# Column sums by 32x32 transposes, fewer norm sums, a new opening and end, and one weight sum moved from VectorE to GpSimd in an encoder block

## Chip, cores and metric

The kernel runs on one core of a Trainium2 chip. The metric is the device time of one execution in microseconds (us). PE is TensorE, DVE is VectorE, ACT is ScalarE, POOL is GpSimd, SP is SyncE, which issues most DMAs.

## What is computed

One block of an encoder on x (1024 positions x 1024 channels, float32), conditioned by a vector c:

```python
ada = silu(c) @ w_ada + b_ada                     # 1024 -> 6 x 1024
shift1, scale1, gate1, shift2, scale2, gate2 = split(ada, 6)
h = rmsnorm(x, g_mix) * (1 + scale1) + shift1
qa, ka, va, qb, kb, vb, ga, gb = split(h @ w_in)  # 512 x6, 1024 x2
oa = mixture_of_dilations(qa, ka, va, rel_bias)   # branch A, 3 window patterns
ob = neighbourhood_attention_2d(qb, kb, vb, rpb)  # branch B
x = x + gate1 * ((sigmoid(ga) * (oa @ w_branch_dil) + sigmoid(gb) * (ob @ w_branch_na)) @ w_out)
h2 = rmsnorm(x, g_ffn) * (1 + scale2) + shift2
u_val, u_gate = split(depthwise_conv3(h2 @ w_up))
x = x + gate2 * ((gelu(u_gate) * u_val) @ w_down)
return rmsnorm(x, g_final)
```

with rmsnorm(x, g) = x * rsqrt(mean(x*x) + 1e-6) * g.

## The kernel before

Activations lie with channels on the partitions: a tile is 128 channels x 512 positions, eight channel tiles (index k or m) by two halves of the positions (`hf`). Every large product is made of three fp32r matmuls: weights and activations are split into a high part (an ACT copy to fp32r, `whi`, `h`) and a low part (a subtraction on POOL or DVE, `wlo`), and high x high, high x low and low x high are added up in PSUM. So PE does most of the work, and ACT, DVE and POOL make its operands.

The stages, in order: the opening (norm of x's first half, the first columns of ada, products for q, k, v of the first heads); v and q/k products of the second half, with the remaining columns of ada summed beside them; attention, where the projections of later heads are woven between the softmax and value matmuls; the gating of the two branches (`w_br`); `w_out` with the norm for the FFN; `w_up` with seven products per 2x2 blocks (Strassen's scheme; `STEPS`, the sums of weights S1 to S4 and of activations T1 to T4), convolution and gelu; `w_down`; and the end with the last norm.

**Column sums.** Sums over partitions are done by PE: `add_sums` (L104) takes a 128x512 tile of squares as the stationary operand, in four blocks of 128 columns, and a column of ones as the moving one; four plain fp32 matmuls (eight records in the trace) give 512 sums, one per position, laid over the partitions. `rstd_of` (L110) makes the reciprocal root of them (DVE, ACT, DVE), and `bcast` (L118) turns it by four transposes into a 128x512 tile `pbc` that DVE multiplies with. Where squares are kept in two accumulators, there are two sets of four. The norm of half 1 does so (`square`, `square_sums`, L201 to L217), `out_tile` for half 0 (its last square apart), and the end (`late`: the sum, m=6 and m=7).

The columns of ada come the same way: `row_pairs` (L555) multiplies rows of `w_ada` by elements of silu(c) and adds them up on DVE into `sums[j]` (a 128x512 tile for each j from 4 to 9, whose 128 partitions are still to be summed), and two steps later `ada_sums` (L170) sums over the partitions with four matmuls against ones, and `ada_bias` (L177) adds the bias on DVE. In the `w_br` stage `row_add` (L1205) does the same for j = 10 and 11.

**Opening.** `warm` issues filler matmuls (L246) until the first data are there. DVE computes 1/D * sum + eps, ACT the root, DVE the reciprocal; ACT copies the turned factor to SBUF (`pbs`), so that POOL may scale x tiles 2 to 7 while DVE scales 0 and 1. The order of all engines in this stage is the order of the code (`manual_schedule`).

**k eviction.** `k_evict` (L370) copies k from PSUM for two heads: `one` is ACT's scaled copy (L381), `two` DVE's low part (L385) and the DMAs to the other 64 partitions. In attention both are put on a list of side work by `later` with a credit in ns, and are issued between the steps of the softmax: scores plus bias on DVE with the row maximum (L672), exp on ACT (L673), turning on PE, copies of the turned tile on ACT (L680, `th`) and DVE (L681, `tl`), then PE again (L795 for the first pattern). In branch B the two heads are put as `later(750, one for head 0)` and `later(750, one for head 1, two for both heads)`. Weight splits (L730 on ACT, L731 on POOL) are side work as well.

**w_up's first tiles.** Each step's weights go through `a_operands` (L1261), a generator: POOL makes S1, S2 and S3 (L1273 to L1275), ACT and POOL split the pairs, DVE makes S4 = a12 - S2 (L1291). `gens` holds the product generators of the first three tiles; the first products need only half 0 of the activations, while half 1 is normed: L113, `bcast` (L121), then DVE scales `m2[k]` (L1640), and forms the sums for T2, T1 and so on (L1643 on) in an order that is written out by hand for ACT, DVE and POOL.

**End.** Three chunks (half 0, and two quarters) get their last products, squares (ACT, L1794), sums on POOL for m < 6 (L1798), `add_sums`, `rstd_of`, `bcast`; a chunk's scaling (L1775) is done in the next chunk's loop. For the last chunk DVE scales all eight tiles (L1814), and four DMAs of 256 KB store them (L1819).

## Time and profile before

| | us |
|---|---|
| median of 3 runs | 1493.36 (1491.71 to 1493.61) |
| profiled execution: its own time | 1490.45 |
| its span in the trace | 1488.6 |
| mean granted TensorE clock | 0.996 |
| DVE / ACT / POOL busy | 935.8 / 773.6 / 763.2 |

In a row of the timeline stand the start, the duration of the group of like instructions (x gives their count), the engine, the line, the operation with its output and inputs, and in brackets the idle time ahead of it and what ended it. Matmuls overlap, so their cadence is read from their starts. In a row of the stages stand the length, then for PE, weight loads, DVE, ACT and POOL the busy time and the count, then the granted clock, the share of the DMA engines and GB/s. A row of groups ends with busy time and mean duration in ns.

### The profile page before, as it was taken

To read this page: it belongs to the slowest core of one execution; us is meant where nothing else is said; L and a number is where in the kernel's file an instruction comes from. 1 tells how busy PE (TensorE), PEld (TensorE's weight loads), DVE (VectorE), ACT (ScalarE), POOL (GpSimd) and SP (SyncE) were. 2 spreads that over 40 slices of the span, in tenths; PEclk is the share of its full clock that TensorE was granted. 3 is DMA by queue.
4 is the path that set the end of the run, shared out by engine and by line. 5 is a ranking of instruction groups with operands and counts; after the bars stand their busy time and mean duration, and the time that the engine had idled before them with its cause. 6 is when DMAs were issued, how large, how long until landed. Compare 5 with 4: busy or idle time off the path is not lost.

```text
span 1488.6 us, 21635 instructions
## 1 busy us (share of the span) xinstructions
PE 1471.5 (99%) x7652; PEld 1252.7 (84%) x7652; DVE 935.8 (63%) x1760; ACT 773.6 (52%) x1442; POOL 763.2 (51%) x635
## 2 busy tenths in 40 slices
PE   9999999999999999999999999999999999999997
PEld 8888888889798998888888778888888888878887
DVE  7783546555555666566515897666666667887865
ACT  5522666666655666653345464444444447485542
POOL 4131332433234354422268668766766676988711
PEclk9999999999999999999999999999999999999998
DMA  9587233445645556577544314222222234542313
GB/s 367 195 303 258 73 97 87 139 108 140 160 148 140 152 156 170 164 259 254 193 152 140 105 43 141 86 85 81 82 70 84 73 133 141 198 141 72 110 36 114
DMA packets 117301, 210.29 MB, mean 141 GB/s; under 512 B 42788, under 2 KB 55716, under 8 KB 117156
## 3 DMA queue, kind: packets, MB, share of 16 engines
q1 hardware_dynamic: 115192, 205.95, 43.2%
q10 hardware_dynamic: 2000, 2.95, 0.5%
q8 instruction: 60, 0.98, 0.3%
q14 instruction: 49, 0.40, 0.1%
HBM read 163.58 MB, written 42.66 MB: 139 GB/s over the span
## 4 chain that ended last, share of the span: by engine, by line
PE 86%; DVE 4%; POOL 3%; DMA 2%; issue 2%; ACT 2%; SPq 0%; DVEq 0%; POOLq 0%; ACTq 0%
PE pj L1326 11%; PE pj L1325 11%; PE pj L1324 11%; PE pj L84 11%; PE pj L86 10%; PE pj L85 10%; PE pj L414 3%; PE O L1027 2%; PE T L1014 1%; PE S L992 1%; PE pv L289 1%; PE pv L291 1%; PE pv L290 1%; PE O L858 1%; PE O L807 1%
## 5 line engine op out<-in xcount | busy, mean ns | idle before, releaser
L61 POOL TENSOR_TENSOR wlo<-wraw,whi 128x512 fp32r<-128x512 f32 (+1 forms) x84 | 106.2, 1287 | 146.1 <-ACT whi L57 145.9
L84 PE MATMUL pj<-h,whi 128*128 128x512 f32 x432 | 178.3, 413 | 0.1
L86 PE MATMUL pj<-h,wlo 128*128 128x512 f32 x432 | 170.0, 394 | 0.0
L85 PE MATMUL pj<-h,whi 128*128 128x512 f32 x432 | 169.6, 392 | 0.0
L1324 PE MATMUL pj<-op,wsh 128*128 128x512 f32 x408 | 159.1, 391 | 1.4 <-ACT op L1254 0.6
L1325 PE MATMUL pj<-op,wsh 128*128 128x512 f32 x408 | 159.0, 390 | 0.9 <-DVE op L1255 0.6
L1326 PE MATMUL pj<-op,wsl 128*128 128x512 f32 x408 | 157.6, 389 | 0.0
L681 DVE TENSOR_TENSOR tl<-T,th 128x512 fp32r<-128x512 f32 (+3 forms) x120 | 77.2, 654 | 106.7 <-ACT th L680 105.4
L731 POOL TENSOR_TENSOR wlo<-wraw,whi 128x512 fp32r<-128x512 f32 x58 | 74.3, 1294 | 125.7 <-ACT whi L730 125.7
L61 POOL TENSOR_TENSOR wsl<-big,wsh 128x512 fp32r<-128x512 f32 (+1 forms) x86 | 111.8, 1323 | 42.5 <-ACT wsh L57 37.6
L673 ACT ACTIVATE P<-P,st 128x256 f32<-128x256 f32 x128 | 64.2, 502 | 93.3 <-DVE st L672 93.3
L1561 DVE SCALAR_TENSOR_TENSOR big<-pj,sm,big 128x512 f32<-128x512 f32 (+2 forms) x183 | 94.9, 563 | 16.5 <-ACT big L1555 15.6
L86 PEld LDWEIGHTS pj<-h,wlo 128*128 128x128 f32 x432 | 81.1, 188 | 18.0
L1324 PEld LDWEIGHTS pj<-op,wsh 128*128 128x128 f32 x408 | 76.6, 188 | 19.3 <-ACT wsh L57 1.5
L1325 PEld LDWEIGHTS pj<-op,wsh 128*128 128x128 f32 x408 | 76.6, 188 | 18.1 <-DVE op L1255 1.2
L84 PEld LDWEIGHTS pj<-h,whi 128*128 128x128 f32 x432 | 81.6, 189 | 11.5 <-issue 0.5
L1325 PE MATMUL pj<-op,whi 128*128 128x512 f32 x232 | 90.4, 390 | 0.0
L1326 PE MATMUL pj<-op,wlo 128*128 128x512 f32 x232 | 90.3, 389 | 0.0
L1324 PE MATMUL pj<-op,whi 128*128 128x512 f32 x232 | 90.2, 390 | 0.0
L85 PEld LDWEIGHTS pj<-h,whi 128*128 128x128 f32 x432 | 81.8, 189 | 10.0
L1326 PEld LDWEIGHTS pj<-op,wsl 128*128 128x128 f32 x408 | 76.6, 188 | 16.0 <-POOL wsl L61 0.3
L61 POOL TENSOR_TENSOR wsl<-wraw,wsh 128x384 fp32r<-128x384 f32 (+1 forms) x46 | 57.3, 1268 | 62.0 <-ACT wsh L57 54.5
(403 smaller groups left out, 4171.7 us busy)
## 6 DMA issues: line engine op xcount, KB each, us to landing
wraw<-w_in SPq DMA_DIRECT2D x32, 512.0 KB
wada<-w_ada SPq DMA_DIRECT2D x31, 512.0 KB
big<-w_up SPq DMA_DIRECT2D x22, 512.0 KB
wraw<-w_up SPq DMA_DIRECT2D x22, 512.0 KB
big<-as SPq DMA_DIRECT2D x22, 512.0 KB
as<-big SPq DMA_DIRECT2D x21, 512.0 KB
gs<-gs SPq DMA_DIRECT2D x32, 256.0 KB
g<-gs SPq DMA_DIRECT2D x16, 512.0 KB
```

The costliest lines, as they stand in the source:

```text
L61: lo_eng.tensor_tensor(lo[:, i:i + step], raw[:, i:i + step], f(hi)[:, i:i + step], OP.subtract)
L84: pe.matmul(psum, whi[:, k0 + k], mhi, start=k == 0, stop=False)
L85: pe.matmul(psum, whi[:, k0 + k], mlo, start=False, stop=False)
L86: pe.matmul(psum, wlo[:, k0 + k], mhi, start=False, stop=k == n - 1)
L414: pe.matmul(p[:, 256 * r:256 * r + 256], ww[:, k], m[:, r], start=k + x + r == 0, stop=k == KT - 1 and x == 2, skip_group_check=True)
L673: act.activation(pp, pp, AF.Exp, bias=mi, scale=-1.0, accum_out=li)
L681: dve.tensor_tensor(tl[:m, :n], pt[:m, :n], f(th)[:m, :n], OP.subtract)
L731: pool.tensor_tensor(lo[:, i:i + n], raw[:, i:i + n], f(hi)[:, i:i + n], OP.subtract)
L1324: pe.matmul(psum, whi[:, k], bhi, start=j < 4 and k == 0, stop=False, skip_group_check=True)
L1325: pe.matmul(psum, whi[:, k], blo, start=False, stop=False, skip_group_check=True)
L1326: pe.matmul(psum, wlo[:, k], bhi, start=False, stop=k == n - 1, skip_group_check=True)
L1561: dve.scalar_tensor_tensor(y[:, dst], src, wt, y[:, dst], OP.mult, OP.add)
```

## The change

1. Column sums of ada (j = 4 to 9 and 10, 11): the partitions are summed in two steps. `fold` turns the 128x512 sum in 32x32 blocks on DVE (a transpose) and reduces the 32 elements of each block's rows to one (128x16). `folds_in` makes a 128x32 matrix `pick` once, by a reduce over the identity. `fold_bias` sums the four groups of 32 partitions with four matmuls, for all six j at once (32x24) at the end of the stage, or for one j (32x4) in `w_br`. The adds of the bias become one for j = 4 to 9.
2. Norms: the squares of half 1 in the early stage go into one accumulator (one set of four matmuls instead of two), as do those of half 0 in `w_out` (one DVE add more for m = 7) and m = 6 at the end for the first two chunks.
3. Opening: 35 filler matmuls instead of 38; eps is a tile, added by the root's bias on ACT, so that DVE's scaling of the sum goes; ACT copies the turned factor ahead of the second half of a weight split; DVE scales x tile 1 behind the first bias.
4. `k_evict` in branch B: `two` is split by head, with a further entry of credit 400.
5. `w_up`: tile 1's S4 is made by POOL, ahead of the split of S3; the factor of half 1 is turned as soon as tile 0's products are issued that far, not three steps of tile 1 later.
6. End: eps as the root's bias; for the last chunk the factor is turned a second time into `bc2`, ACT copies it to SBUF and scales x tiles 4 and 5, POOL multiplies these two, DVE scales the other six; tiles 6 and 7 are stored one by one, and ACT's queue stores 4 and 5.

The core of the diff:

```diff
+    def fold(dst, acc, tmp):
+        dve.transpose(tmp, acc)
+        dve.tensor_reduce(dst, tmp.rearrange("p (c i) -> p c i", i=32), mybir.AxisListType.X, OP.add)
+    def folds_in(tile, n):
+        pick, sums = tile[:, 0:32], tile[:, 32:32 + 16 * n].rearrange("p (j x) -> p j x", j=n)
+        dve.tensor_reduce(pick, idt.rearrange("p (b i) -> p i b", i=32), mybir.AxisListType.X, OP.add)
+        return pick, sums
+    def fold_bias(c0, n, pa, pick, sums):
+        for q in range(4):
+            pe.matmul(pa[32 * q:32 * q + 32, :4 * n], pick, sums.rearrange("p j (m q) -> p (j m) q", q=4)[:, :, q],
+                      start=True, stop=True, skip_group_check=True)
+        ada_bias(c0, pa, 4 * n)
...
-            later(750, lambda: one((1,)), two)
+            later(750, lambda: one((1,)), lambda: two((0,)))
+            later(400, lambda: None, lambda: two((1,)))
...
-        warm(38, idle, True)
+        warm(35, idle, True)
...
-        dve.tensor_scalar(r, every(pcol), 1.0 / D, EPS, OP.mult, OP.add)
-        act.activation(r, r, AF.Sqrt)
+        act.activation(r, every(pcol), AF.Sqrt, bias=eps, scale=1.0 / D)
...
-        pcol = square_sums(accs, lambda: v_products(1, (1,), range(8)))
+        v_products(1, (1,), range(8))
+        pcol = ps_n.tile([128, KT], FT, name="pcol")
+        add_sums(pcol, sqa, True, True)
...
+                if i == 3:
+                    fold(folds[1][:, j - 4], sums.pop(j), early.tile([128, 512], FT, name="mt", bufs=3))
...
-            for j in due.pop(n, ()):
-                ada_bias(4 * j, ada_sums([(sums.pop(j), ones)]))
-            due[n + 2] = [j for j in range(4, 10) if done_rows < 4 * j - 12 <= row_ends[n]]
...
-        for j in sum(due.values(), []):
-            ada_bias(4 * j, ada_sums([(sums.pop(j), ones)]))
+        fold_bias(16, 6, ps_s.tile([128, 512], FT, name="pada", bufs=1), *folds)
...
+        if s4_at == 3:
+            pool.tensor_tensor(S4, a12, S2, OP.subtract)
...
-        if 0 < m < KT - 1:
-            (dve if hf and m > 2 else pool).tensor_tensor(sqa, sqa, sq, OP.add)
+        if 0 < m < KT - 1 or m and hf == 0:
+            (dve if hf and m > 2 or m == KT - 1 else pool).tensor_tensor(sqa, sqa, sq, OP.add)
...
-    prep.append(a_operands(raw.pop(1), 4, s_home, sts[1], dve, spot=extra))
+    prep.append(a_operands(raw.pop(1), 4, s_home, sts[1], dve, spot=extra, s4_at=3))
...
     advance(gens[0])
-    for _ in range(3):
-        next(gens[1])
     bc = bcast(rstd_of(pcol, 4), ps, "pbc")
...
-                elif m < 6:
+                elif m < (7 if cs.start == 0 else 6):
                     pool.tensor_tensor(sqa, sqa, sq, OP.add)
...
+            act.activation(r, pcol[:, :n // 128], AF.Sqrt, bias=eps, scale=1.0 / D)
+            dve.reciprocal(r, r)
...
+        bc2 = bcast(r, ps, "pj", 2, 6)[:, :n]
...
+        for m in (4, 5):
+            act.activation(xs[m], xs[m], AF.Copy, scale=g_fin[:, m:m + 1])
+        act.activation(bs, bc2, AF.Copy)
...
+        for i in range(2):
+            pool.tensor_tensor(ys[4][:, i], xs[4 + i], bs, OP.mult)
...
+        for m in (0, 1, 2, 3, 6, 7):
...
+            dve.scalar_tensor_tensor(yy, xs[m], g_fin[:, m:m + 1], bc, OP.mult, OP.mult)
```

What this moves on the engines, at three places. First, DVE at the end of the early stage, where it sums the last rows of ada (`sq` is such a sum, `wada` the rows); before:

```order
L567 SCALAR_TENSOR_TENSOR sq_1170<-wada_1122,cs_65,sq_1170 128x512 x2
L565 TENSOR_SCALAR sq_1243<-wada_1126,cs_65 128x512
L567 SCALAR_TENSOR_TENSOR sq_1243<-wada_1126,cs_65,sq_1243 128x512
L567 SCALAR_TENSOR_TENSOR sq_1243<-wada_1164,cs_65,sq_1243 128x512 x2
L177 TENSOR_TENSOR ada_70<-pada_1251,sm_64 128x4
L567 SCALAR_TENSOR_TENSOR sq_1243<-wada_1168,cs_65,sq_1243 128x512
L1457 TENSOR_TENSOR am1_71<-ada_70 128x4
L567 SCALAR_TENSOR_TENSOR sq_1243<-wada_1168,cs_65,sq_1243 128x512
L567 SCALAR_TENSOR_TENSOR sq_1243<-wada_1173,cs_65,sq_1243 128x512 x2
L177 TENSOR_TENSOR ada_70<-pada_1317,sm_64 128x4
L177 TENSOR_TENSOR ada_70<-pada_1325,sm_64 128x4
L620 SCALAR_TENSOR_TENSOR am2_72<-ada_70,sm_64 128x8
```

and after, with the line numbers of the changed kernel (L575 and L577 are the sums, `mt_821` holds `pick` and the folded sums):

```order
L181 STREAM_TRANSPOSE mt_1233<-sq_1166 128x512
L182 TENSOR_REDUCE mt_821<-mt_1233 128x16
L575 TENSOR_SCALAR sq_1236<-wada_1125,cs_65 128x512
L577 SCALAR_TENSOR_TENSOR sq_1236<-wada_1125,cs_65,sq_1236 128x512
L577 SCALAR_TENSOR_TENSOR sq_1236<-wada_1157,cs_65,sq_1236 128x512 x2
L577 SCALAR_TENSOR_TENSOR sq_1236<-wada_1164,cs_65,sq_1236 128x512 x2
L577 SCALAR_TENSOR_TENSOR sq_1236<-wada_1169,cs_65,sq_1236 128x512 x2
L181 STREAM_TRANSPOSE mt_1273<-sq_1236 128x512
L182 TENSOR_REDUCE mt_821<-mt_1273 128x16
L177 TENSOR_TENSOR ada_70<-pada_1309,sm_64 128x24
L628 SCALAR_TENSOR_TENSOR am2_72<-ada_70,sm_64 128x8
```

Between the sums the small bias adds are gone, a fold (L181, L182) stands behind each finished sum, and one bias add of 24 columns is left. On PE at this place, among the v products (`pv`), before:

```order
L291 MATMUL pv_1361<-vwh_194,h_792 128x512
L289 MATMUL pv_1361<-vwh_194,h_796 128x512
L290 MATMUL pv_1361<-vwl_195,h_796 128x512
L170 MATMUL pada_1325<-ones_68,sq_1243 128x1 x4
L291 MATMUL pv_1361<-vwh_194,h_797 128x512
L289 MATMUL pv_1361<-vwh_194,h_801 128x512
```

and after:

```order
L295 MATMUL pv_1345<-vwh_194,h_785 128x512
L296 MATMUL pv_1345<-vwl_195,h_785 128x512
L297 MATMUL pv_1345<-vwh_194,h_786 128x512
L192 MATMUL pada_1309<-mt_821 32x24 x4
L295 MATMUL pv_1345<-vwh_194,h_790 128x512
L296 MATMUL pv_1345<-vwl_195,h_790 128x512
```

The group L192 needs the last fold; the set it replaces needed the last sum.

Second, DVE in attention, at the k eviction of branch B (`kl` are the low parts of k, `P` the scores); before:

```order
L681 TENSOR_TENSOR tl_4159<-T_4153,th_4158 128x512
L385 SCALAR_TENSOR_TENSOR kl_3687<-pj_4062,ks_3685 64x2x256
L385 SCALAR_TENSOR_TENSOR kl_3688<-pj_4062,ks_3686 64x2x256
L672 ISA P_4179,st_3678<-S_4178,bias_3870 128x256
L672 ISA st_3678 128x1
L672 ISA P_4179,st_3678<-S_4178,bias_3870 128x256
L672 ISA st_3678 128x1
L933 TENSOR_TENSOR u23_2895<-u23_2895,fb_4050 128x512
L681 TENSOR_TENSOR tl_4208<-T_4202,th_4207 128x512
```

and after (L391 is the eviction, L680 the softmax, L689 the turned tile's low part):

```order
L689 TENSOR_TENSOR tl_4143<-T_4137,th_4142 128x512
L391 SCALAR_TENSOR_TENSOR kl_3671<-pj_4046,ks_3669 64x2x256
L680 ISA P_4158,st_3662<-S_4157,bias_3854 128x256
L680 ISA st_3662 128x1
L680 ISA P_4158,st_3662<-S_4157,bias_3854 128x256
L680 ISA st_3662 128x1
L941 TENSOR_TENSOR u23_2879<-u23_2879,fb_4034 128x512
L391 SCALAR_TENSOR_TENSOR kl_3672<-pj_4046,ks_3670 64x2x256
L689 TENSOR_TENSOR tl_4192<-T_4186,th_4191 128x512
```

The second low part stands five rows later, behind a softmax and an add. On ACT at this place (`whi` is a weight split, `th` a turned tile), before:

```order
L381 ACTIVATE ks_3685<-pj_4062 64x2x256
L680 ACTIVATE th_4158<-T_4153 128x512
L381 ACTIVATE ks_3686<-pj_4062 64x2x256
L730 ACTIVATE whi_4145<-wraw_3951 128x512
L673 ACTIVATE P_4179,st_3678<-P_4179,st_3678 128x256 x2
L730 ACTIVATE whi_4145<-wraw_3951 128x512
L680 ACTIVATE th_4207<-T_4202 128x512
```

and after:

```order
L387 ACTIVATE ks_3669<-pj_4046 64x2x256
L688 ACTIVATE th_4142<-T_4137 128x512
L387 ACTIVATE ks_3670<-pj_4046 64x2x256
L681 ACTIVATE P_4158,st_3662<-P_4158,st_3662 128x256 x2
L738 ACTIVATE whi_4129<-wraw_3935 128x512 x2
L688 ACTIVATE th_4191<-T_4186 128x512
```

Both halves of the weight split stand together ahead of the next turn copy.

Third, PE at the first tiles of w_up, where the factor of half 1 is turned (`pj` are products, `rs` the factor); before:

```order
L1324 MATMUL pj_8639<-op_7864,whi_8605 128x512
L1325 MATMUL pj_8639<-op_7864,whi_8605 128x512
L1326 MATMUL pj_8639<-op_7864,wlo_8606 128x512
L121 MATMUL pbc_8653<-idt_63,rs_8649 128x128 x4
L1324 MATMUL pj_8639<-op_7865,whi_8605 128x512
L1325 MATMUL pj_8639<-op_7865,whi_8605 128x512
L1326 MATMUL pj_8639<-op_7865,wlo_8606 128x512
```

and after:

```order
L1339 MATMUL pj_8610<-op_7859,whi_8516 128x512
L1340 MATMUL pj_8610<-op_7859,whi_8516 128x512
L1341 MATMUL pj_8610<-op_7859,wlo_8517 128x512
L121 MATMUL pbc_8633<-idt_63,rs_8629 128x128 x4
L1339 MATMUL pj_8638<-op_7856,whi_8596 128x512
L1340 MATMUL pj_8638<-op_7856,whi_8596 128x512
L1341 MATMUL pj_8638<-op_7856,wlo_8597 128x512
```

The turn stands ahead of the new tile's products instead of behind nine of them. On POOL there (`xb` holds S1 and S2, `wsl` low parts), before:

```order
L1273 TENSOR_TENSOR xb_8601<-wraw_8599 128x512
L1274 TENSOR_TENSOR xb_8601<-xb_8601,wraw_8597 128x512
L1275 TENSOR_TENSOR wraw_8599<-wraw_8597,wraw_8599 128x512
L61 TENSOR_TENSOR wsl_8610<-xb_8601,wsh_8609 128x512 x2
L61 TENSOR_TENSOR xb_8894<-wraw_8597,xb_8894 128x512
```

and after:

```order
L1285 TENSOR_TENSOR xb_8592<-wraw_8590 128x512
L1286 TENSOR_TENSOR xb_8592<-xb_8592,wraw_8588 128x512
L1287 TENSOR_TENSOR wraw_8590<-wraw_8588,wraw_8590 128x512
L1307 TENSOR_TENSOR wraw_8588<-wraw_8588,xb_8592 128x512
L61 TENSOR_TENSOR wsl_8601<-xb_8592,wsh_8600 128x512 x2
L61 TENSOR_TENSOR xb_8885<-wraw_8588,xb_8885 128x512
```

The S4 sum (L1307) stands ahead of the weight splits.

More of the change, by code (lines that the diff above doesn't have):

```diff
@@ L199, in x_load, with square @@
         return x
[L201 to L204 removed]
+    def square(x, acc, ks, e):
         for k in ks:
[L206 to L207 removed]
+            sq = early.tile([128, 512], FT, name="mt", bufs=3) if k else acc
             act.activation(sq, x[k], AF.Square)
[L209 removed]
+            if k:
                 e.tensor_tensor(acc, acc, sq, OP.add)
[L212 to L217 removed]
     def norm_bcast(pcol):
@@ L590, in hybrid_encoder @@
         done_rows = 0
-        due = {}
+        folds = folds_in(early.tile([128, 512], FT, name="mt", bufs=3), 6)
         for n, step in enumerate(v_steps[:10]):
@@ L1214, in row_add @@
             sums[j] = dst
+        if t == KT - 1:
+            folds = folds_in(opool.tile([128, 512], FT, name="oraw", bufs=6), 1)
+            fold(folds[1][:, 0], dst, opool.tile([128, 512], FT, name="oraw", bufs=6))
+            return lambda: fold_bias(4 * j, 1, ps.tile([128, 512], FT, name="pbc"), *folds)
+        return lambda: None
     row_load(0)
@@ L1233, in hybrid_encoder @@
             row_load(i + 1)
-        row_add(i)
+        then = row_add(i)
         p = []
@@ L1238, in hybrid_encoder @@
             product(p[br], ws[m], lambda k: [t[:, k, cols] for t in o[br]], 4 * br, 4)
-        if i % 8 == 7:
-            j = late[i][0]
-            ada_bias(4 * j, ada_sums([(sums.pop(j), ones)], new=ps.tile([128, 512], FT, name="pbc")))
+        then()
         g = gates.pop(i)
@@ L1259, in hybrid_encoder, with a_operands @@
     names = tuple(b for _, b in STEPS)
-    def a_operands(raw, n, work, st, lo_eng=pool, last=False, w_at=0, spot=None, apart=False):
+    def a_operands(raw, n, work, st, lo_eng=pool, last=False, w_at=0, spot=None, apart=False, s4_at=0):
         spot = spot or big
@@ L1287, in a_operands @@
         yield
+        if s4_at == 2:
+            pool.tensor_tensor(S4, a12, S2, OP.subtract)
         pair(ws, ("S2", "S1"), *s_tiles())
-        S4 = S1 if apart else a12
-        if w_at != 3:
+        if w_at != 3 and not s4_at:
             dve.tensor_tensor(S4, a12, S2, OP.subtract)
         yield
+        if s4_at == 3:
+            pool.tensor_tensor(S4, a12, S2, OP.subtract)
         pair(raw[1], ("S3", "22"), *s_tiles())
```

68 lines of the change are left out of this document (31 added, 37 removed).

## Prediction

> **What bounds the kernel now.** I read the page's busy times first, then the chain that ended last, then busy time by stage, then TensorE's waits.
>
> ```profile
> PE   1471.5 (99%) x7652; PEld 1252.7 (84%) x7652; DVE 935.8 (63%) x1760; ACT 773.6 (52%) x1442; POOL 763.2 (51%) x635
> PE 86%; DVE 4%; POOL 3%; DMA 2%; issue 2%; ACT 2%; SPq 0%; DVEq 0%; POOLq 0%; ACTq 0%
> 200.00:400.00 200.00, 197.49 (x1195) 172.75 (x1194) 110.31 (x323) 128.58 (x329) 70.14 (x63) 0.99 0.44 122
> 840.00:1000.00 160.00, 156.29 (x682) 127.28 (x681) 127.60 (x192) 77.57 (x100) 108.96 (x81) 1.00 0.23 78
> 1400.00:1488.60 88.60, 80.93 (x475) 71.58 (x473) 52.89 (x94) 29.29 (x56) 24.86 (x26) 0.96 0.22 73
> PE pj L321 <- ACT h L239: 0.7, 1, 0.7
> ```
>
> TensorE (PE) is busy for 1471.5 of 1488.6 us. So a change gains in two ways only: fewer PE instructions, or one of the few gaps closed: 2.5 us in 200 to 400, 3.7 in 840 to 1000, and 7.7 at the end (first two numbers of each row). What the other engines save elsewhere is worth nothing.
>
> **Column sums on PE.** Price of one set, from PE's timeline:
>
> ```profile
> 102.97 0.39 PE L291 MATMUL pv<-vwh,h 128*128 128x512 f32 x1
> 103.19 0.95 PE L170 MATMUL pada<-ones,sq 128*128 128x1 f32 x8
> 104.33 0.40 PE L290 MATMUL pv<-vwl,h 128*128 128x512 f32 x1
> 104.56 0.40 PE L291 MATMUL pv<-vwh,h 128*128 128x512 f32 x1
> ```
>
> From 102.97 to 104.56 PE starts one set of ones-matmuls and three wide matmuls. Wide ones start 0.23 apart, so the set costs 1.59 - 3 x 0.226 = 0.91 us, although it moves one column. Before attention seven sets go (six of L170, one in the norm of half 1): 7 x 0.91 = 6.4. One group of four matmuls (L192 after) comes. No row shows its form, with weights 32 columns wide; between a quarter and the whole of a set (0.2 to 0.9), I take half, 0.45.
>
> On VectorE (DVE) each of six rows gets a fold: a transpose of 128x512 and a reduce. No row shows either, so I bound an operation by the nearest rows:
>
> ```profile
> 122.75 5.52 DVE L567 SCALAR_TENSOR_TENSOR sq<-wada,cs,sq 128x512 f32<-128x512 f32 x6 [10.83 <-DMA wada<-w_ada]
> 128.18 0.48 DVE L565 TENSOR_SCALAR sq<-wada,cs 128x512 f32<-128x512 f32 x1
> 133.12 1.54 DVE L567 SCALAR_TENSOR_TENSOR sq<-wada,cs,sq 128x512 f32<-128x512 f32 x2 [0.52 <-DMA wada<-w_ada]
> 138.74 0.95 PE L170 MATMUL pada<-ones,sq 128*128 128x1 f32 x8
> 89.52 5.06 DVE L567 SCALAR_TENSOR_TENSOR sq<-wada,cs,sq 128x512 f32<-128x512 f32 x3
> 92.30 1.74 POOL L61 TENSOR_TENSOR vwl<-wraw,vwh 128x512 fp32r<-128x512 f32 x1
> 96.20 0.88 DVE L61 TENSOR_TENSOR vwl<-qs,vwh 128x512 fp32r<-128x512 f32 x1
> ```
>
> One input takes 0.48, two inputs about 0.77 (1.54 / 2), and beside a busy GpSimd (POOL) 1.69 (5.06 / 3, as long as POOL's own 1.74). So a fold takes 0.96 to 3.4; I take 1.25, since POOL has little to do when the late ones run. The early folds lie beside PE work. Two places wait. PE needs a low part that DVE makes (96.20 row, ends 97.08) and came for it 0.7 later than that; with two sets gone ahead of it PE comes 1.8 earlier. Part of what DVE does there follows PE and so moves too; how much no row tells, I take 1.0, which leaves a wait of about 0.2 (0 to 1.1). Then the group: PE comes to it at 138.15 - 5.4 = 132.8 (the last set at 138.74 less the matmuls moved behind it, less six sets). DVE ended at 134.66; it starts about 1.0 earlier, takes two folds more (+2.5), and loses three column adds of 0.15 and most of the 0.52 that it waited for a transfer (-0.8): 135.4. PE waits 2.6. Term: 6.4 - 0.45 - 0.2 - 2.6 = **3.1**. If nothing waits, 5.9; if folds take 3.4 and PE's clock falls for the longer wait (below), 3.1 - 4.3 - 1.7 = -2.9.
>
> In w_br two sets become groups of four: 2 x (0.91 - 0.45) = **0.9** (0 to 1.4). Their folds fit into an idle DVE of 2.8 us:
>
> ```profile
> 694.18 0.16 DVE L177 TENSOR_TENSOR ada<-pbc,sm 128x4 f32<-128x4 f32 x1 [2.78 <-PE pbc L170]
> ```
>
> In w_out one set goes for one DVE add beside PE work: **0.9**. In the end part one set of four and one of two go: 0.91 + 0.5 = **1.4**; the added POOL add hides behind matmuls.
>
> **The one stall in attention.** Timeline at the k eviction of branch B, and busy time around it:
>
> ```profile
> 388.86 2.24 DVE L385 SCALAR_TENSOR_TENSOR kl<-pj,ks 64x512 fp32r<-64x512 f32 x2 [0.41 <-ACT ks L381]
> 392.59 0.61 ACT L730 ACTIVATE whi<-wraw 128x512 fp32r<-128x512 f32 x1
> 393.23 0.60 ACT L680 ACTIVATE th<-T 128x512 fp32r<-128x512 f32 x1
> 393.86 0.69 DVE L681 TENSOR_TENSOR tl<-T,th 128x512 fp32r<-128x512 f32 x1 [1.35 <-ACT th L680]
> 394.61 0.44 PE L795 MATMUL T<-idt,P 128*128 128x128 f32 x2 [2.51 <-DVE tl L681]
> 395.00:396.00 1.00, 1.00 (x6) 0.85 (x5) 0.23 (x2) 1.00 (x4) 0.00 (x0) 0.72 0.78 160
> 396.00:398.00 2.00, 2.00 (x9) 1.73 (x8) 0.93 (x3) 1.87 (x5) 0.00 (x0) 0.50 0.13 45
> 398.00:400.00 2.00, 2.00 (x10) 1.79 (x10) 1.85 (x6) 0.74 (x3) 0.00 (x0) 0.79 0.13 51
> 869.00:874.00 5.00, 3.32 (x15) 2.44 (x14) 5.00 (x8) 1.48 (x3) 2.91 (x2) 1.00 0.00 0
> ```
>
> Two k evictions in a row hold DVE for 2.24, the softmax behind them is late, ScalarE (ACT) turns the scores late, PE idles 2.5. Behind the stall the granted clock (third number from the end) is 0.72, 0.50 and 0.79: 0.28 + 1.0 + 0.42 = 1.7 us more. In 869 to 874, with 1.68 idle, it stays 1.00. The change puts the second eviction behind the softmax, 1.1 sooner; but ACT now has both weight splits (0.61 each) ahead of the turn copy instead of one. Net 0.5 off the stall, leaving 2.0, near the gap that kept its clock: 0.5 + 1.7 = **2.2** (0 to 4.2).
>
> [...]
>
> **w_up's first tiles.**
>
> ```profile
> 831.07 2.28 DVE L61 TENSOR_TENSOR wlo<-wraw,whi 128x1024 fp32r<-128x1024 f32 x1
> 834.58 1.29 POOL L1274 TENSOR_TENSOR xb<-xb,wraw 128x512 f32<-128x512 f32 x1
> 835.62 0.60 PE L121 MATMUL pbc<-idt,rs 128*128 128x128 f32 x4
> 835.90 1.77 DVE L1291 TENSOR_TENSOR wraw<-wraw,xb 128x512 f32<-128x512 f32 x1 [2.03 <-POOL xb L1274]
> 837.59 1.27 DVE L1640 TENSOR_TENSOR x<-x,pbc 128x512 f32<-128x512 f32 x2
> 840.00:860.00 20.00, 18.47 (x77) 13.96 (x76) 19.58 (x28) 11.22 (x18) 5.33 (x4) 1.00 0.09 27
> 860.00:880.00 20.00, 17.82 (x78) 14.12 (x77) 20.00 (x26) 9.91 (x15) 12.73 (x9) 1.00 0.11 34
> L1640 DVE TENSOR_TENSOR x<-x,pbc 128x512 f32<-128x512 f32 x8 | 5.3, 677 | 0.0
> L1643 DVE TENSOR_TENSOR big<-x,big 128x512 f32<-128x512 f32 x2 | 1.9, 934 | 0.0
> ```
>
> From 837.6 to 880 DVE is never idle and PE waits for it: 1.53 + 2.18 = 3.7 us. The S4 sum (1.77) leaves DVE, which had stood idle 2.03 ahead of it, and the turned factor comes nine matmuls (2.0 us) sooner, at once behind the reciprocal (about 833.9): the scaling starts at about 834.6, three us sooner. That could close all of 3.7. Against it: the sum (1.29 on POOL, by the 834.58 row) stands ahead of POOL's weight splits, which then come 1.3 late for PE. I take half, **1.8** (-1.3 to 3.7).
>
> [...]
>
> **Opening and tail.**
>
> ```profile
> 22.85 1.30 ACT L57 ACTIVATE vwh<-kl 128x512 fp32r<-128x512 f32 x2 [1.60 <-DMA kl<-w_in]
> 1477.40 0.74 POOL L1798 TENSOR_TENSOR wc<-wc 128x256 f32<-128x256 f32 x1
> 1480.61 0.16 DVE L113 TENSOR_SCALAR rs<-pcol 128x2 f32<-128x2 f32 x1 [0.42 <-PE pcol L108]
> 1482.10 3.22 DVE L1814 SCALAR_TENSOR_TENSOR wc<-x,sm,pbc 128x256 f32<-128x256 f32 x8 [0.90 <-PE pbc L121]
> ```
>
> The opening can close PE's wait of 0.7 (first block), but at 22.85 ACT waits for a transfer that nothing here moves, so I give **0.1** (0 to 0.6); three filler matmuls less only move where PE waits. The copy of the turned factor now stands ahead of two weight splits on ACT, and the constant for the root is set on DVE and POOL in idle stretches: nothing, and at most 0.6 if the splits come late, which takes the 0.1 away. At the end the DVE step ahead of the root goes (0.16, and its signal to ACT: 0.2) and DVE scales six tiles instead of eight (3.22 / 4 = 0.8): **1.0** (0.2 to 1.8). POOL's two (2 x 0.74, on tiles that ACT has scaled before) start behind ACT's copy of the second turned factor and end about with DVE's six (6 x 0.40); without that cover the 0.8 is gone. The last tiles now leave one by one; if that saves as much again, 1.8.
>
> **Sum:** 3.1 + 0.9 + 0.9 + 1.4 + 2.2 + 1.8 + 0.1 + 1.0 = 11.4. The profiled execution took 1490.45, so 1479.0 for its like; the median of the runs is 2.9 above it, so the forecast is **1482.0**.
>
> **Rivals.**
> - Folds are slow (3.4 each, lockstep with POOL) and PE's longer wait halves its clock: 11.4 - 4.3 - 1.7 = 5.4, so **1488.0**. For: the 89.52 row. Against: the fold has one input.
> - The waits bind anyway: attention, w_up and the first column sums gain nothing, since what PE then waits for (transfers, DVE, ACT) did not move: 0.9 + 0.9 + 1.4 + 0.1 + 1.0 = 4.3, **1489.1**; at the low ends of these, within 0.2%.
> - All waits vanish (group in time 2.6, the other half of w_up 1.9, the rest of the stall 2.0): 17.9, **1475.5**.
> - The clock drop isn't due to the stall: 11.4 - 1.7, **1483.7**.
> - Slower: seven other k evictions of branch B are split too, each with another ACT and DVE order. Where the turn copy then comes last, a stall like that at 394 opens (2.5 + 1.7 = 4.2). From four such sites on the time is over that of before; four give 11.4 - 16.8, **1498.8**. Against: before, only one of the eight sites shows a wait.
>
> **How the numbers follow.** Forecast 0.47, slow folds 0.12, binding waits 0.14, all vanish 0.08, clock 0.12, slower 0.07. Some 0.2% (3 us) is what a measurement of this kernel tells from no change. The range runs from 1475.5, the best case, to 1490.0, above the binding waits; outside lie the slower case, part of the binding waits and the tails. Faster 0.85 (half the binding waits taken off, some more from elsewhere), same 0.08, slower 0.07.
>
> **What would show it.** PE's busy time about 9 us lower; no sets of eight one-column records before 140; a PE wait of 2 to 3 us at the new group near 133; a wait of about 2 at L795's place and no clock under 1.00 behind it; DVE's scaling in w_up starting three us sooner after the reciprocal, with less PE idle in the 40 us behind it. A clock of 0.5 behind the group, or waits at other k evictions, would make the forecast wrong.

## The result, and the profile after

The changed kernel takes 1487.79 us (median of 11 runs, 1484.40 to 1491.25), the kernel before in the same sessions 1492.32 us (11 runs, 1489.25 to 1495.40). The ratio is 0.9963, 95% interval 0.9951 to 0.9976: 5.5 us faster (3.6 to 7.3), half of the 11.4 that were forecast. The profiled execution took 1484.40 us and is the fastest of the eleven; its span is 1482.6 us, 6.0 less than before.

The page's busy row, busy time from 200 to 400 us, and PE's two longest waits, of the changed kernel:

```profile
PE 1461.3 (99%) x7580; PEld 1243.2 (84%) x7580; DVE 945.5 (64%) x1770; ACT 774.0 (52%) x1445; POOL 766.9 (52%) x641
200.00:400.00 200.00, 195.06 (x1184) 170.88 (x1183) 107.90 (x318) 127.16 (x325) 69.91 (x63) 0.98 0.42 118
PE pj L84 <- DVE kl L391: 4.9, 1, 4.9
PE pada L192 <- DVE mt L182: 2.7, 1, 2.7
```

PE is busy 10.2 us less than before (1471.5 to 1461.3), but the span shrank by 6.0 only. Between 200 and 400 us 4.9 us are idle where it was 2.5, and a wait of 2.7 at the new group of matmuls is there. So work went, and stalls came.

Where it went is read by setting the starts of the same matmuls side by side in both traces; the difference at a few places, and what each stretch gained (us; negative is a loss):

| stretch (time in the trace before) | forecast | gained |
|---|---|---|
| opening, to 53 | 0.1 | -0.2 |
| column sums before attention, 53 to 146 | 3.1 | 1.4 |
| attention with the k eviction, 146 to 453 | 2.2 | -2.3 |
| rest of attention and w_br, 453 to 770 | 0.9 | 1.5 |
| w_out, to 830 | 0.9 | 0.9 |
| w_up's first tiles, 830 to 880 | 1.8 | 2.6 |
| 880 to 1430 | 0 | 0.7 |
| sums at the end, to the last products | 1.4 | 1.3 |
| tail, to the end of the span | 1.0 | 0.1 |
| sum | 11.4 | 6.0 |

**The group.** DVE's and PE's timeline, and busy time behind it:

```profile
127.50 0.71 DVE L181 STREAM_TRANSPOSE mt<-sq 128x512 f32<-128x512 f32 x1
128.25 0.69 DVE L182 TENSOR_REDUCE mt<-mt 128x16 f32<-128x512 f32 x1
134.87 0.71 DVE L181 STREAM_TRANSPOSE mt<-sq 128x512 f32<-128x512 f32 x1
135.62 0.69 DVE L182 TENSOR_REDUCE mt<-mt 128x16 f32<-128x512 f32 x1
136.36 0.32 PE L192 MATMUL pada<-mt 128*32 128x24 f32 x8 [2.69 <-DVE mt L182]
136.50:138.00 1.50, 1.50 (x11) 1.22 (x9) 0.42 (x3) 0.00 (x0) 0.46 (x1) 0.50 0.77 177
138.00:140.00 2.00, 2.00 (x7) 1.56 (x6) 0.00 (x0) 0.45 (x1) 0.00 (x0) 0.66 1.01 222
```

A fold takes 1.44 us (127.50 to 128.94; DVE starts its next row 1.35 behind the fold's start; 1.25 was assumed). PE is free at 133.67 (136.36 - 2.69), DVE ends the last fold at 136.31, and PE has waited 2.69. What the forecast left out stands in the last two rows: the granted clock is 0.50 and 0.66 for 3.5 us, 0.75 + 0.68 = 1.4 us more (wide products start 0.43 us apart there, 137.63 to 138.06, and 0.23 ahead of the wait, 132.82 to 133.05).

**The k eviction.** SP's queue and DVE's add in the kernel before:

```profile
365.47 12.02 SPq L428 DMA_DIRECT2D v<-vbc  x16
382.82 1.13 SPq L927 DMA_DIRECT2D fb<-fcs  x2
391.82 0.69 DVE L933 TENSOR_TENSOR u<-u,fb 128x512 f32<-128x512 f32 x1
```

and SP, DVE and PE in the changed kernel, with busy time behind the stall:

```profile
367.77 12.03 SPq L435 DMA_DIRECT2D v<-vbc  x16
385.19 1.12 SPq L935 DMA_DIRECT2D fb<-fcs  x2
392.99 0.69 DVE L941 TENSOR_TENSOR u<-u,fb 128x512 f32<-128x512 f32 x1 [4.58 <-DMA fb<-fcs]
393.72 1.06 DVE L391 SCALAR_TENSOR_TENSOR kl<-pj,ks 64x512 fp32r<-64x512 f32 x1
394.83 0.79 PE L84 MATMUL pj<-h,whi 128*128 128x512 f32 x1 [4.94 <-DVE kl L391]
394.00:396.00 2.00, 1.17 (x3) 0.97 (x4) 1.97 (x5) 0.13 (x1) 0.00 (x0) 0.50 1.06 205
396.00:398.00 2.00, 2.00 (x9) 1.60 (x8) 0.26 (x3) 1.95 (x7) 0.00 (x0) 0.50 0.36 79
```

The second low part (L391, 393.72) stands behind the add L941, which waits 4.58 us for the transfer into `fb`. PE needs the `pj` buffer that L391 reads for its next product, and waits 4.94. Before, DVE reached this add only after both low parts, at 391.82, and the transfer was there (no idle time stands in its row). SP issues it behind sixteen small transfers that take 12 us of its queue (L435 now, L428 before), at 385.19, not earlier than before (382.82), although PE is 1.2 us ahead here. The clock is 0.50 when PE goes on.

### The profile page after: what moved, and what is told of

The parts are those of the page before. It is cut to its first block, busy times and chain, and to the rows that moved or that the text cites. A ratio compares the mean times of both kernels' runs of the same rounds, so it can differ in the third digit from the quotient of the medians.

```text
span 1482.6 us, 21512 instructions
## 1 busy us (share of the span) xinstructions
PE 1461.3 (99%) x7580; PEld 1243.2 (84%) x7580; DVE 945.5 (64%) x1770; ACT 774.0 (52%) x1445; POOL 766.9 (52%) x641
## 4 chain that ended last, share of the span: by engine, by line
PE 84%; DVE 6%; DMA 5%; issue 1%; POOL 1%; ACT 1%; SPq 1%; DVEq 0%; ACTq 0%; POOLq 0%
PE pj L1339 11%; PE pj L1340 11%; PE pj L1341 11%; PE pj L84 11%; PE pj L86 11%; PE pj L85 11%; PE pj L421 3%; PE O L1035 2%; PE T L1022 1%; DMA wada<-w_ada 1%; PE S L1000 1%; PE O L866 1%; DVE sq L577 1%; PE O L815 1%; PE T L803 1%
## 5 line engine op out<-in xcount | busy, mean ns | idle before, releaser
L689 DVE TENSOR_TENSOR tl<-T,th 128x512 fp32r<-128x512 f32 (+3 forms) x120 | 77.1, 654 | 104.4 <-ACT th L688 103.2
```

Source lines behind the costliest of these rows:

```text
L689: dve.tensor_tensor(tl[:m, :n], pt[:m, :n], f(th)[:m, :n], OP.subtract)
```

## The experiments

All ratios are to the kernel before, with 95% intervals. By the widths of these intervals, two versions differ clearly only from about 0.0017 (2.5 us) on.

### The k eviction undone, and alone

The changed kernel with the old eviction (`k_old`), and the old kernel with the new one (`k_alone`):

```diff
-            later(750, lambda: one((1,)), lambda: two((0,)))
-            later(400, lambda: None, lambda: two((1,)))
+            later(750, lambda: one((1,)), two)
```

> The changed kernel with the k eviction of branch B as it was before (both low parts together). Theory 1: the split is what costs, since the second low part now stands on DVE behind the add of L941, which waits for the transfer into fb; PE waits 4.9 us for it and runs at half clock behind. Undoing the split brings the old stall back (2.5 us and 1.7 of clock) in place of 4.9 and about 1.9: 2.6 us faster than the changed kernel, 0.9945 of the kernel before. Theory 2: the 4.9 us are that one execution's slow transfer and not the split's place: no wait of this kind in other executions, time as the changed kernel, 0.996.

> The kernel before with the split k eviction alone. Theory 1: 2.6 us slower than before (1.0017), with a wait of PE for DVE's second low part near 394 of about 5 us. Theory 2: the split takes the old stall of 2.5 us away or shortens it, 2 us faster or nothing (0.9985 to 1.000).

Measured: `k_old` 0.9957 (0.9946 to 0.9969), `k_alone` 1.0001 (0.9991 to 1.0011). The waits and the clock, of `k_old` first:

```profile
PE T L802 <- DVE tl L688: 2.5, 1, 2.5
393.00:395.00 2.00, 1.12 (x7) 1.04 (x8) 1.50 (x6) 0.90 (x4) 1.31 (x1) 1.00 1.02 195
395.00:397.00 2.00, 1.44 (x9) 1.05 (x9) 0.76 (x2) 1.95 (x6) 0.00 (x0) 1.00 1.06 203
```

```profile
PE pj L84 <- DVE kl L385: 2.8, 1, 2.8
```

The old stall comes back with the old code (2.5 us), and the new one comes with the new code alone (2.8 at 393.9): the split takes one stall away and makes another, in either kernel. So the mechanism of `k_old`'s theory 2 (one execution's slow transfer) is out, although its time, 0.996, is what came. `k_alone` came out at the upper end of its theory 2, since its new stall is about as long as the old one (2.84 for 2.51, with a mean clock of 0.97 from 370 to 425 us in both): its add waited 1.76 us for the transfer, not 4.58. Theory 1's time did not come in either run: 1.0017 was expected of `k_alone`, and `k_old` is 0.9 us faster than the changed kernel by the ratios, well within the intervals.

By the traces the stretch from 303 to 453 us costs 2.3 us more than before in the changed kernel, 0.7 in `k_old`, nothing in `k_alone`. From 303 to 410 us `k_old` gains 2.9 on the changed kernel, near the 2.6 expected. By 430 it has given back 1.3: its third add waits 5.29 us for its transfer at 412.07, and a low part behind it holds PE for 0.95. And behind `k_old`'s stall of 2.48 us the clock stayed at 1.00, where it was 0.50 behind the 2.51 of the kernel before (from 396 to 398 us); no run tells why.

### The add one slot later

```diff
-                at(s0 + 24 + 2 * n, "last", self.weigh, g, z)
+                at(s0 + (25, 27, 29, 30)[n], "last", self.weigh, g, z)
```

> The changed kernel with the adds of L941 (multiplication by fb) one slot later each (25, 27, 29 and 30 instead of 24, 26, 28 and 30), so that the second low part stands ahead of the one that waits for its transfer. Theory 1: the wait of 4.9 us at 394 goes or falls below 2, the clock stays near 1.00 there: 5 us faster than the changed kernel, 0.9930 of before. Theory 2 (the split's place has nothing to do with it): 0.996. Rival within theory 1: the turn copies on ACT, with both weight splits ahead, still hold PE for 2 us, and the clock falls: 0.9945.

Measured: 0.9949 (0.9937 to 0.9961), 2.1 us faster than the changed kernel by the ratios. PE's waits, and DVE and PE at the fourth add:

```profile
PE O L866 <- DVE tl L689: 1.9, 1, 1.9
PE T L803 <- DVE tl L689: 1.1, 1, 1.1
PE pada L192 <- DVE mt L182: 2.8, 1, 2.8
420.86 0.69 DVE L941 TENSOR_TENSOR u<-u,fb 128x512 f32<-128x512 f32 x1 [5.03 <-DMA fb<-fcs]
423.05 0.39 PE L866 MATMUL O<-tl,vv 128*128 128x256 f32 x1 [1.85 <-DVE tl L689]
```

The wait for L391 is gone from the list, so the add did hold it. At 410 us this kernel is 4.8 us ahead of the changed one, so theory 1 holds at its place (5 expected), with 1.1 of waiting left there for a turned tile, whose copy on ACT DVE waits for. By 430 us it has given back 2.7: the fourth add, which the edit moves too, waits 5.03 us for its transfer, and a low part behind it holds PE for 1.85. So the same mechanism sits at a later add, and the rival (ACT's turn copies hold PE for 2 us, and the clock falls) is not what took the rest: the mean clock from 370 to 425 us is 1.00.

### The small transfers earlier

```diff
-    at(52, "first", vb_chunks)
+    at(49, "first", vb_chunks)
```

> The changed kernel with sixteen small transfers of v (L435 on SP's queue) issued three slots earlier (49 instead of 52), which puts them ahead of the factors' transfers instead of between the factors' arithmetic and the first of them. DVE's order at the k eviction is unchanged. Theory 1: the wait of L941, and behind it of the second low part and of PE, comes from SP's queue, which issues these sixteen for 12 us while the factors are ready; with them out of the way fb lands some 4 us or more sooner, DVE doesn't wait at L941, and PE's wait of 4.2 to 4.9 us goes: 4 to 6 us faster than the changed kernel. Theory 2: the transfers themselves are slow there (the DMA engines are full around 390), so the wait stays above 3 us.

In this kernel branch B's v is written over branch A's before A's last heads have read theirs, so part of the output is computed from other values; the work is the same. Measured: 0.9971 (0.9959 to 0.9984), no faster than the changed kernel. SP's transfer into `fb`, DVE's add, and PE's wait:

```profile
386.25 1.12 SPq L935 DMA_DIRECT2D fb<-fcs  x2
396.32 0.68 DVE L941 TENSOR_TENSOR u<-u,fb 128x512 f32<-128x512 f32 x1
PE pj L84 <- DVE kl L391: 1.7, 2, 1.1
```

This execution is some 5 us behind the kernel before from its opening on. Set against PE's products at 384 us, SP issues the transfer about 6 us sooner than in the changed kernel. The add no longer waits: at 396.32 no idle time stands ahead of it. PE's waits for L391 are 1.7 in two pieces instead of 4.9. That part of theory 1 holds: SP's queue made the wait. The 4 to 6 us did not come: between 375 and 402 us PE now waits in five small pieces (0.34 to 1.10, 3.1 in all), and the stretch from 303 to 453 still loses 0.5 against the kernel before (the changed kernel 2.3). At 53 us this execution is already 4.6 us behind the kernel before (the changed kernel 0.2), with PE waiting for an ACT tile, which the move doesn't touch. The profiled execution of `group_small`, the other kernel with this edit, shows the same (4.9); why was not tried.

### The group later, and what the folds are worth

`group_late` issues the group behind the last two v products:

```diff
-        folds = folds_in(early.tile([128, 512], FT, name="mt", bufs=3), 6)
+        folds = folds_in(work.tile([128, 128], FT, name="folds", bufs=1), 6)
...
-        fold_bias(16, 6, ps_s.tile([128, 512], FT, name="pada", bufs=1), *folds)
-        dve.scalar_tensor_tensor(am2, ada[:, 32:40], 1.0, g_ffn, OP.add, OP.mult)
...
         v_out(br, st, *v_wide(st))
+    fold_bias(16, 6, ps_s.tile([128, 512], FT, name="pada", bufs=1), *folds)
+    dve.scalar_tensor_tensor(am2, ada[:, 32:40], 1.0, g_ffn, OP.add, OP.mult)
```

> The changed kernel with the group of four matmuls for ada 16 to 39 (and what follows from it) issued behind the last two v products, 30 matmuls (6.8 us) later; the folded sums lie in another pool. Theory 1: PE's wait of 2.7 us at the group and the half clock behind it (1.4 us) are lost time that nothing takes up later; both go, 4 us faster than the changed kernel, 0.9935 of before. Rival: the stage behind waits for the same sums or for the pool's release, and the wait moves on: less than 1 us faster, 0.996.

`ada_old` takes the folds of j = 4 to 9 out of the changed kernel (`fold`, `folds_in` and `fold_bias` there) and puts back `ada_sums` two steps after each sum:

> The changed kernel with the column sums of ada 16 to 39 as before (six sets of four matmuls against ones, no folds); the norm of half 1 keeps its one set. Theory 1: the six sets cost 0.91 to 1.0 each (5.7), the group that stands for them cost 2.7 of waiting, 1.0 to 1.5 of half clock and 0.3 itself, so by the trace this kernel is only 1 to 1.7 us slower than the changed one at the end of this stage (146 us in the trace). Theory 2 (the prediction's term): 2.2 us slower, since the clock doesn't fall. If the folds cost more than seen, it is faster.

Measured: `group_late` 0.9942 (0.9930 to 0.9954), 3.1 us faster than the changed kernel by the ratios; `ada_old` 0.9972 (0.9953 to 0.9992). PE at the group in `group_late`:

```profile
139.84 0.39 PE L297 MATMUL pv<-vwh,h 128*128 128x512 f32 x1
140.16 0.28 PE L192 MATMUL pada<-folds 128*32 128x24 f32 x8
140.37 0.50 PE L84 MATMUL pj<-h,whi 128*128 128x512 f32 x1
```

No wait stands ahead of the group, and it costs 0.53 - 0.23 = 0.30 us between its neighbours (0.45 was assumed). Behind it this kernel is 6.0 us ahead of the kernel before and still 5.6 at 186 us, against 1.2 for the changed kernel: 4.4 to 4.8 by the trace, theory 1. `ada_old` is 0.4 ahead at 146 us. So in the changed kernel the folds were worth 0.8 us by these two traces, 0.2 of it already there at 53 us, ahead of the first fold; the second profile of the changed kernel (below) is 0.3 ahead there and puts it at nothing. Theory 2, the prediction's 2.2, is out, and theory 1 of `ada_old` was still too high.

### w_up: the sum's place and the factor's

`s4_on_dve` leaves out `s4_at=3` in tile 1's `a_operands`; `factor_late` puts the three steps back:

```diff
     advance(gens[0])
+    for _ in range(3):
+        next(gens[1])
     bc = bcast(rstd_of(pcol, 4), ps, "pbc")
```

> The changed kernel with tile 1's S4 sum on DVE again. Theory 1: the sum stands ahead of the first scaling on DVE, which then has to wait for POOL's xb and starts about 3 us later; PE's idle time between 840 and 880 goes from 1.9 back towards 3.7 us, 1 to 2 us slower than the changed kernel. Theory 2: turning the factor early is what gains and the sum's place is indifferent: PE idle there stays near 1.9.

> The changed kernel with the factor of half 1 turned behind three more product steps of tile 1, as before (S4 stays on POOL). Theory 1: DVE's scaling starts 2.0 us later, which goes straight into PE's waits between 840 and 880: idle 1.9 becomes 3 to 4, 1 to 2 us slower than the changed kernel. Theory 2: the sum's move alone is the gain, and PE's idle time stays near 1.9.

Measured: 0.9977 (0.9965 to 0.9988) and 0.9982 (0.9970 to 0.9994), 2 and 3 us slower than the changed kernel by the ratios, the first of them within the intervals (by the idle times below 0.6 and 1.5; the rest lies elsewhere in those runs). DVE's scaling and POOL's sum in the changed kernel, then busy time from 840 to 880 of the changed kernel, of `s4_on_dve`, and of `factor_late`:

```profile
833.10 1.28 DVE L1652 TENSOR_TENSOR x<-x,pbc 128x512 f32<-128x512 f32 x2 [0.81 <-PE pbc L121]
835.50 1.74 POOL L1307 TENSOR_TENSOR wraw<-wraw,xb 128x512 f32<-128x512 f32 x1
```

```profile
840.00:860.00 20.00, 19.56 (x87) 15.86 (x85) 19.50 (x27) 12.40 (x19) 8.04 (x6) 1.00 0.09 27
860.00:880.00 20.00, 18.54 (x80) 14.55 (x79) 20.00 (x32) 9.20 (x13) 12.50 (x10) 1.00 0.24 79
```

```profile
840.00:860.00 20.00, 19.10 (x83) 15.30 (x82) 19.50 (x27) 13.08 (x21) 6.18 (x5) 1.00 0.09 27
860.00:880.00 20.00, 18.41 (x79) 14.42 (x79) 20.00 (x31) 7.96 (x12) 12.31 (x9) 1.00 0.26 79
```

```profile
840.00:860.00 20.00, 18.48 (x77) 13.91 (x76) 19.58 (x27) 11.76 (x19) 6.08 (x5) 1.00 0.09 27
860.00:880.00 20.00, 18.11 (x79) 14.20 (x78) 20.00 (x27) 8.96 (x13) 13.32 (x10) 1.00 0.16 53
```

PE's idle time there is 0.44 + 1.46 = 1.9 us in the changed kernel, 0.90 + 1.59 = 2.5 with the sum on DVE, 1.52 + 1.89 = 3.4 with the factor late, and was 3.7 before. So the two depend on each other: with the factor late, the sum's move gains 0.3 of the 1.8, and with the sum on DVE the early factor still gains 1.2. Theory 1 holds for both, with the smaller size for the sum.

### The old tail

The block behind the last `bcast` as before (diff above, read backwards), with the root on ACT kept.

> The changed kernel with the last chunk's scaling and stores as before (all eight tiles on DVE, four stores of 256 KB, no second turned factor); the root with its bias on ACT stays. Theory 1: the 1 MB of stores sets the end, at the rate at which the DMA engines write, from the first store on, and the first store starts at the same distance from the factor: end of sums to end of span the same within 0.3 us, so no change from the changed kernel. Theory 2 (the prediction): two DVE tiles of 0.40 us are on the path, so 0.8 us longer from the end of the sums to the end of the span.

Measured: 0.9974 (0.9958 to 0.9990). The last sums, of the kernel before, the changed kernel and `tail_old`, with the first scaling behind them:

```profile
1478.72 0.95 PE L108 MATMUL pcol<-ones,wc 128*128 128x1 f32 x8
1479.96 0.60 PE L108 MATMUL pcol<-ones,wc 128*128 128x1 f32 x4 [0.30 <-ACT wc L1794]
```

```profile
1473.43 1.50 PE L108 MATMUL pcol<-ones,wc 128*128 128x1 f32 x12 [0.50 <-POOL wc L1812]
1476.07 1.66 DVE L1839 SCALAR_TENSOR_TENSOR wc<-x,sm,pbc 128x256 f32<-128x256 f32 x4 [0.65 <-PE pbc L121]
```

```profile
1475.03 1.50 PE L108 MATMUL pcol<-ones,wc 128*128 128x1 f32 x12 [0.50 <-POOL wc L1812]
1477.67 3.22 DVE L1831 SCALAR_TENSOR_TENSOR wc<-x,sm,pbc 128x256 f32<-128x256 f32 x8 [0.64 <-PE pbc L121]
```

From the end of the sums to the end of the span: before 1488.60 - 1480.56 = 8.04; changed 1482.60 - 1474.93 = 7.67; old tail 1484.20 - 1476.53 = 7.67. Theory 1 holds to the hundredth: six tiles instead of eight on DVE are worth nothing, since the stores set the end. The DMA view of the changed kernel, GB/s in 40 slices of 0.275 us from 1472 on:

```profile
GB/s 7 11 15 175 302 257 242 302 205 328 212 328 220 298 19 0 0 0 0 0 0 182 354 305 339 302 365 339 343 357 332 332 261 4 0 0 0 0 0 0
```

The last stores fill twelve slices, 3.3 us, without a hole, the ten between the first and the last at 302 to 365 GB/s (`tail_old` has the same twelve, at 280 to 358); the first of them is issued 0.9 us behind the first scaling in the changed kernel (1476.97) and in `tail_old` (1478.57) alike. The 0.37 less stands where DVE's step ahead of the root went (0.2 forecast). It is given back ahead of that: from the start of the last product to the end of the sums it was 1480.56 - 1478.60 = 1.96 and is 1474.93 - 1472.65 = 2.28, since all twelve records now wait 0.50 for POOL's sum, and before, eight of them ran at once (1478.72).

### Both stalls moved

`both_moved` is `group_late` with the later add; `group_small` is `group_late` with the earlier transfers (and the same part of the output computed from other values).

> The changed kernel with both moves: the group of four matmuls behind the last v products, and the adds of L941 a slot later. The mechanism found so far (two stalls, each with some half clock behind it) gives the sum of both gains: the traces put 4.6 us on the group's wait and clock and 2.5 to 3.5 on the k eviction, so 7 to 8 us faster than the changed kernel by its trace. Rival: from about 1300 us on, PE running ahead meets POOL waiting for the loads of w_down (2 to 3 us were given back there in the kernels that were ahead), so only 4 to 5 us faster, 0.993 of the kernel before. With the gain kept whole: 0.991.

> The changed kernel with the group of four matmuls late and the sixteen small transfers early, L941 in its own place. By theory 1 as good as or better than the version with both moves (0.9927 of before), since nothing on DVE is put off: 0.992. By theory 2 as the version with the late group alone, 0.994.

Measured: `both_moved` 0.9927 (0.9911 to 0.9944), median 1482.02 us, 5.4 us faster than the changed kernel by the ratios and 10.9 faster than the kernel before: the best version here. `group_small` 0.9956 (0.9940 to 0.9972), no better than `group_late`, so its theory 1 failed. (Its profiled execution, 1490.20 us, is the one with the long opening; the other five lie at 1482.73 to 1484.58, which is no better than `group_late` either.)

At 1253 us in the trace before, `both_moved` is 11.8 us ahead, 7.9 more than the changed kernel: the sum of both gains, and all that was forecast. Between 1270 and 1385 it gives back 2.7, as its rival said. POOL's wait for a load of w_down there, in the changed kernel and in `both_moved`:

```profile
1348.74 1.01 POOL L1285 TENSOR_TENSOR big<-wraw 128x384 f32<-128x384 f32 x1 [0.59 <-DMA wraw<-w_down]
```

```profile
1344.31 1.01 POOL L1285 TENSOR_TENSOR big<-wraw 128x384 f32<-128x384 f32 x1 [2.20 <-DMA wraw<-w_down]
```

The load that POOL's weight sum needs lands 2.20 us late instead of 0.59, then ACT's copy and PE wait (PE 2.1 us in four waits for `wsh`). This was not only for kernels that run ahead: of the other versions all but `k_alone` gave back from 0.1 us (`factor_late`) to 4.0 (`group_small`) there, and 3.2 in `s4_on_dve`, which had been 3.1 ahead.

### The changed kernel once more

> The changed kernel itself once more, for what its executions share. Theory 1: the waits at the group (2.7 us) and at the k eviction (4.2 to 4.9) come again, since they follow from the order on DVE and SP; what differs is the clock behind them, and the 2 to 3 us given back around 1300 to 1360, which the first profile of it did not show (0.7) and six of its variants did. Theory 2: the wait at the k eviction belongs to one execution's transfers and is not there.

One execution, 1488.41 us, beside 1493.94 of the kernel before.

```profile
PE pj L84 <- DVE kl L391: 4.7, 1, 4.7
PE pada L192 <- DVE mt L182: 2.8, 1, 2.8
```

Both waits are there again, and theory 2 is out. From 1270 to 1385 it gives back 2.3 us, though it was only 2.9 ahead; the first profile gained 0.7 there. So the first profile was a lucky one at this place. What makes a load of w_down land late in one execution and in time in another was not settled.

## Why the prediction was right in sign and twice too large

- **Right:** PE's price of a set. Where a set is gone and nothing comes for it, the starts move by 0.9 to 1.0 us, and 0.91 was taken. w_br gives 1.1 at its two sets (0.9), w_out 0.9, the end 1.3 (1.4).
- **Right:** the wait at the group, 2.6 worked out from DVE's rows; 2.69 and 2.81 in the two profiles of the changed kernel. Partly luck: PE came, and DVE was done, 0.9 us later than reckoned (133.7 and 136.3 for 132.8 and 135.4), and the two errors cancel.
- **Wrong:** the same term left out what follows that wait, although the prediction had shown it at 394; it was counted for slower folds only. Behind that wait of 2.7 the clock was 0.50 and 0.66 for 3.5 us, 1.4 us more; a clock of 0.5 behind the group is one of the signs that the prediction itself gave for being wrong. The term was 3.1 and came out as 1.4.
- **Wrong, and the largest:** "The change puts the second eviction behind the softmax ... Net 0.5 off the stall". The order shown ahead of the prediction has the add of L933 (L941 after) between the softmax and the second eviction. It was counted as work on DVE and not as a wait: before, it came with its transfer landed, because two evictions had stood ahead of it. Two things were late next, and neither was looked up: that transfer in SP's queue, and the `pj` buffer that the second eviction holds (PE waited 4.94 us for it). A term of +2.2 came out as -2.3. With the add later (`both_moved`) the stretch gains 1.2, and up to 410 us 2.5, before a later add's transfer holds DVE in the same way. So what failed was the cost of the new order, not the gain of the split.
- **Wrong in size:** the tail. DVE's two tiles were taken as the path; the stores are. 1.0 came out as 0.1: 0.37 behind the sums, and 0.32 lost ahead of their end.
- **Right, and smaller than what came:** w_up, 1.8 forecast. PE's idle time from 840 to 880 went from 3.7 to 1.9, as the term says, and the stretch from 830 on gained 2.6. The scaling starts 0.98 us behind the reciprocal's start (832.12 to 833.10), three us sooner, as said.
- **The rivals.** "Folds are slow" came nearest in time (1488.0), by luck: a fold took 1.44, not 3.4, and only its half about the clock came true. "The waits bind anyway" (1489.1) is the nearer one in mechanism: it held for the k eviction, and almost for the folds, but not for w_up. The slower case did not happen: none of the other seven evictions shows a wait in the first profile.
- **The clock behind the stall.** The prediction left a gap of 2.0 us there and let it keep the clock, as the 1.68 in 869 to 874 had. Whether 2.0 would have kept it no run shows: behind waits of 1.85 and 2.48 us the clock stayed at 1.00, with four of the five of 2.51 to 2.84 in the last section's table it fell, and behind one of 1.79 four products took 1.80 us instead of 1.02. The term that hung on it was lost for another reason. The rival "The clock drop isn't due to the stall" (1483.7) has no run for it: from 370 to 425 us the mean clock was 0.97 before, 0.94 with the wait of 4.94, and 1.00 in `both_moved`, where that stall is gone.

Of the 5.4 us between forecast and the first profile, the k eviction accounts for 4.5, the group for 1.7, the tail for 0.9 and the opening for 0.3; 2.0 came back in w_up and in small amounts elsewhere.

## What to carry to other kernels

When an instruction is moved on an engine that works in order, as DVE does in these rows (the second low part started 0.04 us behind the add that had waited 4.58), look at every row that now stands ahead of it, ask what each of them waits for, and whether the moved one had been hiding that wait; a transfer's landing is looked up in the queue that issues it. A late group of sums gains only if it is put where its operands are long ready: issued 30 matmuls later, the same group gained 4.4 us more by the trace and 3.1 by the times. At the end of a kernel like this one count the stores from the first one on, not the arithmetic that feeds them.

## What the runs showed of the hardware

**PE's waits and the clock then.** In the changed kernel the granted clock was 0.50 for 3.41 us at the group (135.95 to 139.36) and for 6.83 us at the k eviction (391.95 to 398.78); in the kernel before it was 0.50 for 3.41 us at its stall (395.41 to 398.82). Busy time and clock ahead of the fall at the group and at half clock, and two stretches at the same place in `add_late`:

```profile
132.54:135.95 3.41, 1.13 (x5) 0.58 (x4) 3.27 (x5) 1.49 (x2) 0.00 (x0) 1.00 0.54 203
135.95:139.36 3.41, 3.00 (x15) 2.38 (x16) 0.77 (x4) 0.00 (x0) 1.00 (x1) 0.50 0.78 163
132.66:136.07 3.41, 2.15 (x10) 1.46 (x8) 3.27 (x5) 2.09 (x3) 0.00 (x0) 1.00 0.71 261
136.07:139.48 3.41, 1.86 (x15) 1.55 (x16) 1.85 (x6) 0.00 (x0) 1.00 (x1) 1.00 0.43 102
```

In the first stretch of the changed kernel PE is idle for 2.28 us (3.41 - 1.13), and the next one is at half clock. In `add_late` a longer wait, 2.81, lies in the two stretches with 1.26 and 1.55, and the clock stays at 1.00. Waits of PE and the clock that was measured with them:

| wait, us | granted clock then |
|---|---|
| 1.49 (second profile of the changed kernel, 867 us) | 1.00 |
| 1.68 (before, 871 us) | 1.00 |
| 1.79 (`small_early`, opening) | four products behind it took 1.80 us (40.90 to 42.70) instead of 1.02 (21.33 to 22.35) |
| 1.85 (`add_late`, 423 us) | 1.00 |
| 2.48 (`k_old`, k eviction) | 1.00 |
| 2.51 (before, k eviction) | 0.50 |
| 2.69 (changed, group) | 0.50 |
| 2.81 (second profile of it, group) | 0.50 |
| 2.81 (`add_late`, group) | 1.00 |
| 2.84 (`k_alone`, k eviction) | 0.97 as the mean of 370 to 425 us, as with the 2.51 before |
| 3.01 (`group_small`, opening) | 0.50 |
| 4.1 (`ada_old`), 4.72 (second profile), 4.94 (changed), k eviction | 0.50 |

Two equal waits of 2.81 went either way. So the length of one wait did not settle it in these executions; what did was not shown. At the end of the kernel the clock was 0.50 from 1477.4 us on in the changed kernel, with waits of 0.50 and 0.65 ahead, and from 1480.9 in the kernel before, with one of 0.30; no run tells why.

**The new operations.** The 128x512 transpose in 32x32 blocks took 0.71 us on DVE and the reduce of 128x512 to 128x16 0.69, also while POOL made a low part from two tiles (the fold at 88.19 in the changed kernel, POOL busy from 88.33 on). Four fp32 matmuls with 32 weight columns and 24 moving ones cost PE 0.30 us, against 0.91 for four with 128 and one.
